# Where the rotation tables are loaded and worked out, and how the first weights come in, in a decoder block on one core

## The chip, the cores and the metric

The kernel runs on one core of a Trainium2 chip. A core has five engines with a queue of instructions each: TensorE (PE: matrix products and transposes), VectorE (DVE), ScalarE (ACT), GpSimd (POOL) and SyncE (SP, which here only issues DMAs). Engines run on their own and wait for each other by semaphores. The metric is the device time of one execution, in microseconds (us).

## The reference, cut to what matters

One block of a decoder for 1024 tokens of width 1024. Only the beginning of its first part, the two mixers, is touched:

```python
h = rms_norm(x, attn_norm_g)                 # x / sqrt(mean(x*x) + 1e-6) * g
proj = h @ w_in                              # 1024 x 3688, split by columns
dq, dk, dv, iq, ik, iw, cq, ckv, kpe, gd, gm = split(proj)
k_a = rope(rms_norm(dk, dsa_k_g), pos)       # 64 columns, first attention's key
k_i = rope(ik, pos)                          # 64 columns, indexer's key
kv_b = rms_norm(ckv, mla_ckv_g) @ mla_w_ukv  # 128 columns -> 8 heads x (64 + 64)
k_b = rms_norm(concat(k_nope, k_pe), mla_k_g)
def rope(x, pos):                            # rotation by pos * inv_freq
    cos, sin = cos(ang), sin(ang)
    return concat(x1 * cos - x2 * sin, x2 * cos + x1 * sin)
```

Behind it come attention over the 256 best keys, a second causal attention, gates, a cross attention to a memory and a mixture of 16 experts.

## The kernel before, in words

Every float32 product is made of three: each operand is split into a rounded high half (`hi`, ScalarE) and the rest (`lo`, VectorE or GpSimd), and TensorE multiplies hi by hi, hi by lo and lo by hi (`mm3`, L529 to L531).

The first stage is the loop at L809 in `prep`. It goes over eight tiles `i` of 128 tokens, skewed so that each pass works on several tiles at once. Each pass squares the next tile of x on ScalarE (`square_x`, L805), works out reciprocal square roots by three Newton steps in twelve short operations on VectorE (`newton`, L545 to L551), scales the tile (`xn`, L815), and transposes it in two halves on TensorE (L607), each split into `hT_hi` and `hT_lo` (L516, L517). One pass later `project` multiplies tile `i-1` by the 360 weight columns of the first chunk in 24 matmuls of 360 columns, and ScalarE copies the result out (`ev`, L766) and takes its squares (L831 to L834). Three passes behind, the columns of the keys are scaled and rotated with the tables of that tile (`tabs`, L771; `rope_on`, L723 to L726, on GpSimd), duplicated (`kd`, L852), transposed (L859, L861) and split (`cT`, `ks`, `ik`). Four passes behind, `cT` is multiplied by `mla_w_ukv` and copied to `kvb` (L876), and its squares are summed (L878, L879). Those sums, and the sums of the squares of `ev`, share the Newton chain of a later tile of x: `newton` of pass `i` takes eleven columns, of which the first belongs to x of tile `i`, two to `ev` of tile `i-3` and eight to `kvb` of tile `i-6`. So the scaling of tile 6 of x waits for the `kvb` of tile 0.

The 360 columns lie in three pieces of `w_in` (128, 72 and 160 columns). `chunk` loads them in 24 DMAs of 128 rows on SyncE's queue into four buffers `wr` in turn (L559), rounds on ScalarE (L520) and takes the rest on GpSimd (L521). The tables (`tables`, L661 to L719) are cosine and sine of position times frequency, with and without the gains `g_k`, `g_q`, `g_mk`, `g_mq`; they are written to memory as `d_tab` and read back tile by tile. Their small inputs are loaded on SyncE's queue in the middle of, and behind, the weight loads.

The code is written in the order of the loop. A scheduler then puts each engine's instructions into an order by estimated readiness; `issue_after(ins)` keeps instructions that are written inside it behind `ins`. Loads on SyncE's and ScalarE's queue take eight semaphores in turn: a load waits until the load that used its semaphore before has landed.

Of the kernel before, what the change touches and what calls it, by code (L numbers as in the profile page):

```python
# [9 lines left out]
F32 = mybir.dt.float32  # L10
F32R = mybir.dt.float32r
BF16 = mybir.dt.bfloat16
I32 = mybir.dt.int32
AF = mybir.ActivationFunctionType
OP = mybir.AluOpType
# [4 lines left out]
S, D, T, KD = 1024, 1024, 8, 8  # L20
# [478 lines left out]
class Hybrid:  # L499
# [9 lines left out]
    def row(self, name, off, n, tname, pool=None):  # L509
        t = (pool or self.cst).tile([128, n], F32, name=tname)  # L510
        src = self.I[name]
        self.nc.sync.dma_start(t, bass.AP(tensor=src.tensor, offset=src.offset + off, ap=[[0, 128], [1, n]]))
        return t

    def split(self, hi, lo, src):
        self.nc.scalar.activation(hi, src, AF.Copy)  # L516
        self.nc.vector.tensor_sub(lo, src, hi.bitcast(F32))  # L517

# [83 lines left out]
    def transpose_rows(self, xn, hi, lo):  # L602
        for h in range(2):
            p = self.tp().rearrange("p (a b) -> p a b", a=4)
            for i in range(4):
                k = 4 * h + i
                self.nc.tensor.transpose(p[:, i, :], xn[:, k * 128:(k + 1) * 128], self.ident)  # L607
            self.split(hi[:, 4 * h:4 * h + 4], lo[:, 4 * h:4 * h + 4], p)
# [52 lines left out]
    def tables(self, pool):  # L661
        nc, I = self.nc, self.I
        G = nc.gpsimd
        pi = pool.tile([128, T], I32, name="pos_i")
        p = I['positions']
        nc.sync.dma_start(pi, bass.AP(tensor=p.tensor, offset=p.offset, ap=[[1, 128], [128, T]]))
        inv = self.row('inv_freq', 0, 32, "inv", pool)
        gq = self.row('dsa_q_norm_g', 0, 64, "g_q", pool)
        nc.vector.tensor_scalar_mul(gq, gq, -0.125)
        gk = self.row('dsa_k_norm_g', 0, 64, "g_k", pool)  # L670
        mq = self.row('mla_q_norm_g', 64, 32, "g_mq", pool)
        mk = self.row('mla_k_norm_g', 64, 32, "g_mk", pool)
# [3 lines left out]
        ang, k = ak[:, 0], ak[:, 1]  # L676
# [51 lines left out]
    def prep(self):  # L728
# [8 lines left out]
        ikst = (hp.tile([128, S], F32R, name="ik_hi"), hp.tile([128, S], F32R, name="ik_lo"))  # L737
# [5 lines left out]
        W = I['w_in'][0]  # L743
# [47 lines left out]
        def load_x(t):  # L791
            xt[t] = xp.tile([128, D], F32, name="xt", bufs=3)
            (nc.sync if t < 3 else nc.gpsimd).dma_start(xt[t], I['x'][0, tk(t), :])

        load_x(0)
        grow = self.row('attn_norm_g', 0, D, "grow", xp)
        load_x(1)
# [6 lines left out]
        def square_x(t):  # L804
            A.activation(xj, xt[t], AF.Square, scale=1.0 / 32, accum_out=ms(t)[:, 0:1])  # L805

        A.activation(xj[:, 0:128], self.ident, AF.Square)
        square_x(0)
        for i in range(T + 7):  # L809
            if i + 1 < T:  # L810
                square_x(i + 1)
            y = self.newton(ms(i)[:, 0:11], (128, 11))
            if i < T:
                xn = xp.tile([128, D], F32, name="xn", bufs=2)
                V.scalar_tensor_tensor(xn, xt[i], y[:, 0:1], grow, op0=OP.mult, op1=OP.mult)  # L815
                self.transpose_rows(xn, hT[0][:, :, tk(i)], hT[1][:, :, tk(i)])
                if i + 2 < T:
                    load_x(i + 2)
            if i == 0:
                ws, n = chunk([(512, 640), (1152, 1224), (1480, 1640)])  # L820
                c3 = ExitStack()
                tp_ = c3.enter_context(tc.tile_pool(name="tb", bufs=1, side="right"))
                self.tables(tp_)
                c3.close()
                ukv = [self.wpiece([(I['mla_w_ukv'][0, :, j * 512:(j + 1) * 512], 0)], 512) for j in range(2)]
# [1148 lines left out]
```

## Time and profile before

| | |
|---|---|
| median of 3 runs | 1403.38 us (1400.67 to 1403.90) |
| profiled execution | 1405.94 us, span 1404.2 us |
| mean clock granted to TensorE | 0.953 of full |
| TensorE busy | 1239.8 us (88%) |
| VectorE busy | 949.2 us (68%) |
| ScalarE busy | 807.1 us (57%) |
| GpSimd busy | 436.0 us (31%) |

The span is the time between the first and the last record of the profile; the execution's own time is 1.74 us longer. In the timeline a row is one operation or several of one kind in a row (x2, x3): the start, the time of all of them, the engine, the line, and what they write and read. What stands in square brackets is how long the engine was idle before and what ended that. A `q` behind an engine's name is its queue of DMA issues; such a row is the time of the issue, not that of the transfer.

### The profile page before, as it was taken

The page shows a single profiled execution, that of the slowest core. Times are in us where ns is not written, and L with a number is a line of the kernel's source. Part 1 is how long each engine was busy: PE and PEld are TensorE (multiplying, and loading weights), DVE is VectorE, ACT ScalarE, POOL GpSimd, SP SyncE. Part 2 cuts the span into 40 slices and gives each one's busy share as a digit, 9 for nine tenths or more (in the row PEclk, how much of TensorE's full clock was granted, in tenths as well). Part 3 has the DMA queues.
Part 4 walks back from the last instruction along what each step waited for, and adds up shares of the span by engine and source line. Part 5 has one row for each costly group of instructions (what it writes and reads, how often), then busy time and mean ns, then how long its engine had stood idle before and what let it go on. Part 6 is the DMA issues. An engine that isn't in the chain of part 4 may idle for free.

```text
span 1404.2 us, 20787 instructions
## 1 busy us (share of the span) xinstructions
PE 1239.8 (88%) x6884; PEld 1038.2 (74%) x6885; DVE 949.2 (68%) x1963; ACT 807.1 (57%) x1667; POOL 436.0 (31%) x541
## 2 busy tenths in 40 slices
PE   5789899988899999999998999999999378999893
PEld 4678778777787778888776787787878257788772
DVE  7786865889999578778888465232367735677650
ACT  5453654887672388888998422033455334667652
POOL 4555200528884121221343221221223431111111
PEclk9899999999999999999999999999999689999987
DMA  6564102534334454436221234531021857899972
GB/s 201 144 190 137 42 20 82 156 113 155 125 117 150 153 173 151 142 134 208 69 78 61 75 110 138 199 85 38 31 91 60 293 220 232 278 314 304 277 215 36
DMA packets 145749, 203.54 MB, mean 145 GB/s; under 512 B 69824, under 2 KB 91072, under 8 KB 145632
## 3 DMA queue, kind: packets, MB, share of 16 engines
q1 hardware_dynamic: 137040, 173.22, 38.4%
q0 software_dynamic: 7440, 24.71, 6.5%
q10 hardware_dynamic: 1152, 4.19, 0.7%
q8 instruction: 56, 0.92, 0.3%
q14 instruction: 61, 0.50, 0.1%
HBM read 134.61 MB, written 69.70 MB: 146 GB/s over the span
## 4 chain that ended last, share of the span: by engine, by line
PE 36%; DVE 19%; ACT 12%; DMA 11%; issue 9%; POOL 3%; SPq 0%; DVEq 0%; ACTq 0%; POOLq 0%
PE acc L529 4%; PE acc L530 3%; PE acc L531 3%; PE s L529 3%; PE s L530 3%; PE s L531 3%; DMA dn_raw<-in_moe_w_down_dram 2%; ACT tk_junka L1200 2%; DVE ik_hi L1190 2%; DVE ik_lo L1190 2%; DMA gu_raw<-in_moe_w_up_dram 2%; PE tp L1356 2%; PE s L933 1%; DMA gu_raw<-in_moe_w_gate_dram 1%; PE acc L1370 1%
## 5 line engine op out<-in xcount | busy, mean ns | idle before, releaser
L521 POOL TENSOR_TENSOR wl<-wr,wh 128x512 fp32r<-128x512 f32 (+2 forms) x86 | 109.8, 1294 | 175.0 <-ACT wh L520 125.3
L517 DVE TENSOR_TENSOR PT_lo<-tp,PT_hi 128x512 fp32r<-128x512 f32 x152 | 101.6, 685 | 27.4 <-ACT PT_hi L516 26.2
L529 PE MATMUL s<-hT_hi,wh 128*128 128x512 f32 x256 | 102.9, 402 | 3.7 <-ACT s L1061 3.7
L1743 POOL DMA_INDIRECT out_dram<-ey,etok x24 | 39.5, 1644 | 210.4 <-ACT ey L1758 60.0
L531 PE MATMUL s<-hT_hi,wl 128*128 128x512 f32 x256 | 102.0, 401 | 1.7 <-POOL wl L521 1.7
L1726 DVE TENSOR_TENSOR gu_lo<-gu_raw,gu_hi 128x1024 fp32r<-128x1024 f32 x60 | 71.7, 1220 | 44.7 <-ACT gu_hi L1725 42.5
L530 PE MATMUL s<-hT_lo,wh 128*128 128x512 f32 x256 | 101.9, 401 | 0.0
L516 ACT ACTIVATE PT_hi<-tp 128x512 fp32r<-128x512 f32 x152 | 86.7, 594 | 20.3 <-PE tp L1356 8.5
L1200 ACT ACTIVATE tk_junka<-sc,tk_b 128x512 bf16<-128x512 f32 (+2 forms) x96 | 79.4, 827 | 30.5 <-DVE tk_b L1197 29.6
L520 ACT ACTIVATE wh<-wr 128x512 fp32r<-128x512 f32 (+2 forms) x86 | 50.8, 608 | 77.6 <-PE acc L531 27.7
L529 PE MATMUL acc<-wh,hT_hi 128*128 128x512 f32 (+2 forms) x240 | 86.0, 361 | 10.2 <-ACT ev L766 5.4
L1725 ACT ACTIVATE gu_hi<-gu_raw 128x1024 fp32r<-128x1024 f32 x60 | 62.2, 1056 | 50.6 <-DMA gu_raw<-in_moe_w_gate_dram 19.9
L531 PE MATMUL acc<-wh,hT_lo 128*128 128x512 f32 (+2 forms) x240 | 86.6, 361 | 1.9 <-DVE hT_lo L517 1.9
L530 PE MATMUL acc<-wl,hT_hi 128*128 128x512 f32 (+2 forms) x240 | 85.7, 358 | 0.5 <-POOL wl L521 0.5
L1338 DVE TENSOR_REDUCE low<-s 128x1 f32<-128x256 f32 (+3 forms) x64 | 49.1, 769 | 33.0 <-PE s L1337 32.8
L529 PEld LDWEIGHTS acc<-wh,hT_hi 128*128 128x128 f32 x240 | 47.6, 198 | 17.0 <-ACT hT_hi L516 6.0
L529 PEld LDWEIGHTS s<-hT_hi,wh 128*128 128x128 f32 x256 | 49.5, 193 | 14.2 <-ACT s L1061 4.4
L529 PE MATMUL s<-eT1h,gu_hi 128*128 128x224 f32 (+2 forms) x192 | 54.2, 282 | 5.4 <-DVE ewt L1689 3.4
L531 PEld LDWEIGHTS s<-hT_hi,wl 128*128 128x128 f32 x256 | 49.4, 193 | 12.0 <-POOL wl L521 2.1
L942 DVE SCALAR_TENSOR_TENSOR sc<-rel,iw,sc 128x384 f32<-128x384 f32 (+5 forms) x42 | 43.2, 1030 | 21.2 <-ACT rel L936 18.0
L530 PEld LDWEIGHTS s<-hT_lo,wh 128*128 128x128 f32 x256 | 49.6, 194 | 10.1
L530 PE MATMUL s<-eT1l,gu_hi 128*128 128x224 f32 (+2 forms) x192 | 54.6, 284 | 0.0
(543 smaller groups left out, 4126.2 us busy)
## 6 DMA issues: line engine op xcount, KB each, us to landing
d_xs<-zero SPq DMA_DIRECT2D x32, 516.0 KB
dn_raw<-in_moe_w_down_dram SPq DMA_DIRECT2D x32, 512.0 KB
gu_raw<-in_moe_w_gate_dram SPq DMA_DIRECT2D x30, 512.0 KB
gu_raw<-in_moe_w_up_dram SPq DMA_DIRECT2D x30, 512.0 KB
wr<-in_w_in_dram SPq DMA_DIRECT2D x48, 256.0 KB
d_g<-s SPq DMA_DIRECT2D x32, 256.0 KB
gt<-d_g SPq DMA_DIRECT2D x16, 512.0 KB
xg<-d_xs SPq DMA_DIRECT2D x13, 512.0 KB
```

The costliest lines, as they stand in the source:

```text
L516: self.nc.scalar.activation(hi, src, AF.Copy)
L517: self.nc.vector.tensor_sub(lo, src, hi.bitcast(F32))
L520: self.nc.scalar.activation(hi, src, AF.Copy)
L521: self.nc.gpsimd.tensor_sub(lo, src, hi.bitcast(F32))
L529: mm(out, a[0], b[0], start=start, stop=False)
L530: mm(out, a[0], b[1], start=False, stop=False)
L531: mm(out, a[1], b[0], start=False, stop=stop)
L1190: V.tensor_scalar(junks[0][:, :(t + 1) * 128], blk(t), b[:, i:i + 1].bitcast(F32), None, op0=op, op1=OP.add, accum_out=cnt[:, i:i + 1])
L1200: A.activation(junka[:, :(t + 1) * 128], blk(t), AF.Sign, bias=b[:, i:i + 1].bitcast(F32), accum_out=cnt[:, i:i + 1])
L1338: nc.vector.tensor_reduce(low[:, b:b + 1], sp[:, 0:nch, 0:w], AX.XY, OP.min)
L1725: A.activation(hi[:, z], raw_z, AF.Copy)
L1726: E.tensor_sub(lo[:, z], raw_z, hi[:, z].bitcast(F32))
```

## The change

- The seven inputs of the tables and of the normalisation (`pos_i`, `inv`, `grow` and four gains) are loaded by ScalarE's DMA queue, first of all on it, instead of SyncE's.
- The weights of the first chunk come in four pieces of 256 rows with three loads each, 12 instead of 24. They land in buffers that are not yet in use for their own purpose (two of `kvb`, and `ik_hi` and `ik_lo`), so none waits for a buffer to come free. The loads of tiles 1 and 2 of x stand between the pieces.
- The lower halves of these weights are taken alternately on GpSimd and VectorE; their rounding stands behind the first square of x.
- The tables are worked out behind the first normalised tile, the Newton steps of tile 1 too; the pieces of `mla_w_ukv` behind the last split of tile 0.

```diff
--- before.py
+++ after.py
@@ -506,15 +506,16 @@
         if self.dbg is not None and name in self.dbg:
             self.nc.sync.dma_start(self.dbg[name], ap)
 
-    def row(self, name, off, n, tname, pool=None):
+    def row(self, name, off, n, tname, pool=None, q=None):
         t = (pool or self.cst).tile([128, n], F32, name=tname)
         src = self.I[name]
-        self.nc.sync.dma_start(t, bass.AP(tensor=src.tensor, offset=src.offset + off, ap=[[0, 128], [1, n]]))
+        (q or self.nc.sync).dma_start(t, bass.AP(tensor=src.tensor, offset=src.offset + off, ap=[[0, 128], [1, n]]))
         return t
 
     def split(self, hi, lo, src):
-        self.nc.scalar.activation(hi, src, AF.Copy)
+        q = self.nc.scalar.activation(hi, src, AF.Copy)
         self.nc.vector.tensor_sub(lo, src, hi.bitcast(F32))
+        return q
 
     def split_pool(self, hi, lo, src):
         self.nc.scalar.activation(hi, src, AF.Copy)
@@ -605,7 +606,8 @@
             for i in range(4):
                 k = 4 * h + i
                 self.nc.tensor.transpose(p[:, i, :], xn[:, k * 128:(k + 1) * 128], self.ident)
-            self.split(hi[:, 4 * h:4 * h + 4], lo[:, 4 * h:4 * h + 4], p)
+            last = self.split(hi[:, 4 * h:4 * h + 4], lo[:, 4 * h:4 * h + 4], p)
+        return last
 
 
     def build(self):
@@ -658,18 +660,20 @@
         nc.vector.tensor_scalar(self.tri3[:, 128:256], jp, 0.0, -NEG, op0=OP.is_gt, op1=OP.mult)
         nc.vector.memset(self.tri3[:, 256:384], -NEG)
 
-    def tables(self, pool):
+    def table_inputs(self, pool, xp):
+        nc, I = self.nc, self.I
+        pi = pool.tile([128, T], I32, name="pos_i")
+        p = I['positions']
+        nc.scalar.dma_start(pi, bass.AP(tensor=p.tensor, offset=p.offset, ap=[[1, 128], [128, T]]))
+        inv = self.row('inv_freq', 0, 32, "inv", pool, nc.scalar)
+        grow = self.row('attn_norm_g', 0, D, "grow", xp, nc.scalar)
+        return grow, [pi, inv] + [self.row(*a, pool, nc.scalar) for a in (('dsa_k_norm_g', 0, 64, "g_k"), ('mla_k_norm_g', 64, 32, "g_mk"), ('dsa_q_norm_g', 0, 64, "g_q"), ('mla_q_norm_g', 64, 32, "g_mq"))]
+
+    def tables(self, pool, inputs):
         nc, I = self.nc, self.I
         G = nc.gpsimd
-        pi = pool.tile([128, T], I32, name="pos_i")
-        p = I['positions']
-        nc.sync.dma_start(pi, bass.AP(tensor=p.tensor, offset=p.offset, ap=[[1, 128], [128, T]]))
-        inv = self.row('inv_freq', 0, 32, "inv", pool)
-        gq = self.row('dsa_q_norm_g', 0, 64, "g_q", pool)
+        pi, inv, gk, mk, gq, mq = inputs
         nc.vector.tensor_scalar_mul(gq, gq, -0.125)
-        gk = self.row('dsa_k_norm_g', 0, 64, "g_k", pool)
-        mq = self.row('mla_q_norm_g', 64, 32, "g_mq", pool)
-        mk = self.row('mla_k_norm_g', 64, 32, "g_mk", pool)
         pf = pool.tile([128, T], F32, name="pos_f")
         nc.vector.tensor_copy(pf, pi)
         ak = pool.tile([128, T * 64], F32, name="ang").rearrange("p (a t f) -> p a t f", a=2, t=T)
@@ -734,7 +738,6 @@
         self.wp = c.enter_context(tc.tile_pool(name="wp", bufs=10))
         hp = c.enter_context(tc.tile_pool(name="hp", bufs=1))
         hT = self.hT = (hp.tile([128, KD, S], F32R, name="hT_hi"), hp.tile([128, KD, S], F32R, name="hT_lo"))
-        ikst = (hp.tile([128, S], F32R, name="ik_hi"), hp.tile([128, S], F32R, name="ik_lo"))
         iw = hp.tile([128, T, 8], F32, name="iw")
         wk = c.enter_context(tc.tile_pool(name="wk", bufs=2))
         cwe = ExitStack()
@@ -792,9 +795,20 @@
             xt[t] = xp.tile([128, D], F32, name="xt", bufs=3)
             (nc.sync if t < 3 else nc.gpsimd).dma_start(xt[t], I['x'][0, tk(t), :])
 
+        c3 = ExitStack()
         load_x(0)
-        grow = self.row('attn_norm_g', 0, D, "grow", xp)
-        load_x(1)
+
+        kcols, kraw = ((512, 640), (1152, 1224), (1480, 1640)), []
+        for h, (pool, nm) in enumerate(((kp, "kvb"), (hp, "ik_hi"), (kp, "kvb"), (hp, "ik_lo"))):
+            raw, o = pool.tile([128, S], F32, name=nm)[:, 0:720].rearrange("p (k n) -> p k n", k=2), 0
+            for a, b in kcols:
+                nc.sync.dma_start(raw[:, :, o:o + b - a], W[h * 256:h * 256 + 256, a:b].rearrange("(k p) n -> p k n", p=128))
+                o += b - a
+            kraw.append(raw)
+            if h % 2:
+                load_x(1 + h // 2)
+        tp_ = c3.enter_context(tc.tile_pool(name="tb", bufs=1, side="right"))
+        grow, tin = self.table_inputs(tp_, xp)
         ckv_row = self.row('mla_ckv_norm_g', 0, 128, "ckv_row", hp)
         cq_row = self.row('mla_cq_norm_g', 0, 256, "cq_row", hp)
         ms = Stats()
@@ -802,27 +816,35 @@
         xj = xp.tile([128, D], BF16, name="xj", bufs=1)
 
         def square_x(t):
-            A.activation(xj, xt[t], AF.Square, scale=1.0 / 32, accum_out=ms(t)[:, 0:1])
+            return A.activation(xj, xt[t], AF.Square, scale=1.0 / 32, accum_out=ms(t)[:, 0:1])
 
         A.activation(xj[:, 0:128], self.ident, AF.Square)
-        square_x(0)
+        first = square_x(0)
         for i in range(T + 7):
             if i + 1 < T:
                 square_x(i + 1)
-            y = self.newton(ms(i)[:, 0:11], (128, 11))
+            with tc.issue_after(last_xn.ins) if i == 1 else nullcontext():
+                y = self.newton(ms(i)[:, 0:11], (128, 11))
             if i < T:
                 xn = xp.tile([128, D], F32, name="xn", bufs=2)
-                V.scalar_tensor_tensor(xn, xt[i], y[:, 0:1], grow, op0=OP.mult, op1=OP.mult)
-                self.transpose_rows(xn, hT[0][:, :, tk(i)], hT[1][:, :, tk(i)])
-                if i + 2 < T:
+                last_xn = V.scalar_tensor_tensor(xn, xt[i], y[:, 0:1], grow, op0=OP.mult, op1=OP.mult)
+                rows_T = self.transpose_rows(xn, hT[0][:, :, tk(i)], hT[1][:, :, tk(i)])
+                if 2 < i + 2 < T:
                     load_x(i + 2)
             if i == 0:
-                ws, n = chunk([(512, 640), (1152, 1224), (1480, 1640)])
-                c3 = ExitStack()
-                tp_ = c3.enter_context(tc.tile_pool(name="tb", bufs=1, side="right"))
-                self.tables(tp_)
+                ws, n = [], 360
+                for k in range(KD):
+                    hi, lo = (self.wp.tile([128, 512], F32R, name=nm)[:, 0:n] for nm in ("wh", "wl"))
+                    with tc.issue_after(first.ins):
+                        A.activation(hi, kraw[k // 2][:, k % 2], AF.Copy)
+                    (V if k % 2 else G).tensor_sub(lo, kraw[k // 2][:, k % 2], hi.bitcast(F32))
+                    ws.append((hi, lo))
+                ikst = tuple(hp.tile([128, S], F32R, name=nm) for nm in ("ik_hi", "ik_lo"))
+                with tc.issue_after(first.ins), tc.issue_after(last_xn.ins):
+                    self.tables(tp_, tin)
                 c3.close()
-                ukv = [self.wpiece([(I['mla_w_ukv'][0, :, j * 512:(j + 1) * 512], 0)], 512) for j in range(2)]
+                with tc.issue_after(rows_T.ins):
+                    ukv = [self.wpiece([(I['mla_w_ukv'][0, :, j * 512:(j + 1) * 512], 0)], 512) for j in range(2)]
             t = i - 1
             if 0 <= t < T:
                 e = ev[t] = project(ws, n, t)
```

How the order of instructions changes shows at three places. In what follows `DMAHW0` to `DMAHW7` are the eight semaphores of the loads, and a name in square brackets is what the instruction waits for.

ScalarE at the program's start, before: the table load of its functions, a short square, the squares of x (`xj<-xt`) and the first roundings (`wh<-wr`).

```order
L807 ACT_TABLE_LOAD
L807 ACTIVATE xj<-ident 128x128 [waits DVE_49]
L805 ACTIVATE xj,ms<-xt 128x1024 [waits DMAHW0_49,Activation_49,Pool_49]
L805 ACTIVATE xj,ms<-xt 128x1024 [waits DMAHW2_49,Activation_49,Pool_49]
L805 ACTIVATE xj,ms<-xt 128x1024 [waits DMAHW5_49,Activation_49,Pool_49]
L520 ACTIVATE wh<-wr 128x360 [waits DMAHW7_49,DMAHW6_49,DMAHW0_49]
L520 ACTIVATE wh<-wr 128x360 [waits DMAHW3_49,DMAHW2_49,DMAHW1_49]
```

ScalarE at the same place, now:

```order
L667 DMA pos_i<-in_positions_dram 128x8x1
L512 DMA inv<-in_inv_freq_dram 128x32
L512 DMA grow<-in_attn_norm_g_dram 128x1024
L512 DMA g_k<-in_dsa_k_norm_g_dram 128x64
L512 DMA g_mk<-in_mla_k_norm_g_dram 128x32 [waits DMAHW1_49]
L512 DMA g_q<-in_dsa_q_norm_g_dram 128x64 [waits DMAHW3_49]
L512 DMA g_mq<-in_mla_q_norm_g_dram 128x32 [waits DMAHW5_49]
L821 ACT_TABLE_LOAD
L821 ACTIVATE xj<-ident 128x128 [waits DVE_49]
L819 ACTIVATE xj,ms<-xt 128x1024 [waits Activation_49,Pool_49]
L839 ACTIVATE wh<-kvb 128x360 [waits DMAHW6_49,DMAHW4_49,DMAHW2_49]
```

Seven loads stand in front of the table load; three of them wait for an earlier load: the fifth for that of the first tile of x on SyncE's queue, the sixth for `inv`, the seventh for `grow`.

VectorE at the end of the first Newton chain, up to the first normalised tile (`xn`), before:

```order
L551 SCALAR_TENSOR_TENSOR rq_y<-rq_t,rq_y 128x11 [waits DVE_49]
L549 TENSOR_TENSOR rq_t<-rq_y 128x11 [waits DVE_49]
L550 SCALAR_TENSOR_TENSOR rq_t<-rq_t,ms 128x11 [waits DVE_49]
L551 SCALAR_TENSOR_TENSOR rq_y<-rq_t,rq_y 128x11 [waits DVE_49]
L815 SCALAR_TENSOR_TENSOR xn<-xt,rq_y,grow 128x1024 [waits DMAHW1_49,DMAHW0_49,DVE_49]
```

VectorE there, now, from the fifth operation of the chain on (`wl` is the lower half of a weight piece):

```order
L840 TENSOR_TENSOR wl<-kvb,wh 128x360 [waits DMAHW4_49,DMAHW6_49,DMAHW2_49,Activation_49]
L551 SCALAR_TENSOR_TENSOR rq_t<-rq_t,ms 128x11 [waits DVE_49]
L552 SCALAR_TENSOR_TENSOR rq_y<-rq_t,rq_y 128x11 [waits DVE_49]
L840 TENSOR_TENSOR wl<-ik_hi,wh 128x360 [waits DMAHW2_49,DMAHW4_49,DMAHW0_49,Activation_49]
L550 TENSOR_TENSOR rq_t<-rq_y 128x11 [waits DVE_49]
L551 SCALAR_TENSOR_TENSOR rq_t<-rq_t,ms 128x11 [waits DVE_49]
L552 SCALAR_TENSOR_TENSOR rq_y<-rq_t,rq_y 128x11 [waits DVE_49]
L550 TENSOR_TENSOR rq_t<-rq_y 128x11 [waits DVE_49]
L551 SCALAR_TENSOR_TENSOR rq_t<-rq_t,ms 128x11 [waits DVE_49]
L552 SCALAR_TENSOR_TENSOR rq_y<-rq_t,rq_y 128x11 [waits DVE_49]
L840 TENSOR_TENSOR wl<-kvb,wh 128x360 [waits DMAHW1_49,DMAHW7_49,DMAHW0_49,Activation_49]
L830 SCALAR_TENSOR_TENSOR xn<-xt,rq_y,grow 128x1024 [waits DMAHW5_49,DVE_49]
```

Three weight splits are set among the short operations in front of the first normalised tile.

ScalarE around the first copy of the rotated key (`kd`) and the first `kvb`, before; the first row is the square of the last tile of x:

```order
L805 ACTIVATE xj,ms<-xt 128x1024 [waits DMASW4_49,Pool_49]
L516 ACTIVATE hT_hi<-tp 128x4x128 [waits PE_49]
L852 ACTIVATE kd<-kd 128x2x64 [waits Pool_49] x2
L516 ACTIVATE cT_hi<-tp 128x128 [waits PE_49] x2
L516 ACTIVATE ks<-tp 128x128 [waits DVE_49] x2
L516 ACTIVATE ik_hi<-tp 128x128 [waits DVE_49] x2
L766 ACTIVATE ev<-acc 128x360 [waits DMAHW1_49,PE_49]
L852 ACTIVATE kd<-kd 128x2x64 [waits Pool_49]
L876 ACTIVATE kvb<-s 128x1024 [waits PE_49]
```

ScalarE there, now:

```order
L516 ACTIVATE cT_hi<-tp 128x128 [waits PE_49]
L769 ACTIVATE ev<-acc 128x360 [waits PE_49]
L516 ACTIVATE ks<-tp 128x128 [waits DVE_49]
L516 ACTIVATE hT_hi<-tp 128x4x128 [waits PE_49]
L853 ACTIVATE s_605,ms<-ev 128x64 [waits Activation_49]
L854 ACTIVATE s_605,ms<-ev 128x128
L856 ACTIVATE s_605,sskpe<-ev 128x32
L516 ACTIVATE ik_hi<-tp 128x128 [waits DVE_49]
L874 ACTIVATE kd<-kd 128x2x64 [waits Pool_49]
L898 ACTIVATE kvb<-s 128x1024 [waits PE_49]
L819 ACTIVATE xj,ms<-xt 128x1024 [waits DMASW4_49]
L516 ACTIVATE hT_hi<-tp 128x4x128 [waits PE_49]
```

The square of the last tile of x (`xj,ms<-xt`) now stands behind the first `kvb`, and the copy of tile 0's key stands some rows ahead of what is shown here, ahead of the square of the seventh tile.

## Rows read from the trace of the kernel before

**Rows 1.** Page, part 1: busy time, share of the span and count.
```profile
PE 1239.8 (88%) x6884; PEld 1038.2 (74%) x6885; DVE 949.2 (68%) x1963; ACT 807.1 (57%) x1667; POOL 436.0 (31%) x541
```

**Rows 2.** Windows of 10 us: length, PE, PEld, DVE, ACT, POOL busy, clock, DMA, GB/s.
```profile
0.00:10.00 10.00, 0.19 (x1) 0.20 (x3) 4.46 (x22) 3.95 (x8) 0.82 (x13) 1.00 0.71 257
...
50.00:60.00 10.00, 9.12 (x40) 8.70 (x41) 3.25 (x11) 4.46 (x14) 5.75 (x24) 0.67 0.36 106
...
80.00:90.00 10.00, 10.00 (x61) 9.39 (x60) 7.12 (x18) 7.40 (x21) 4.98 (x15) 0.98 0.50 120
```

**Rows 3.** Timeline of ScalarE: start, length, line, operation, out<-in, [idle before <-releaser].
```profile
0.76 1.28 ACT L807 ACT_TABLE_LOAD   x1 [0.63 <-PEq L1961]
2.06 0.31 ACT L807 ACTIVATE xj<-ident 128x128 bf16<-128x128 f32 x1
4.83 1.06 ACT L805 ACTIVATE xj<-xt 128x1024 bf16<-128x1024 f32 x1 [2.47 <-DMA xt<-in_x_dram]
...
26.47 0.49 ACT L520 ACTIVATE wh<-wr 128x360 fp32r<-128x360 f32 x1
...
51.79 1.06 ACT L805 ACTIVATE xj<-xt 128x1024 bf16<-128x1024 f32 x1 [4.13 <-DMA xt<-in_x_dram]
...
53.33 0.50 ACT L852 ACTIVATE kd<-kd 128x128 f32<-128x128 f32 x2
...
59.72 1.03 ACT L876 ACTIVATE kvb<-s 128x1024 f32<-128x1024 f32 x1 [0.73 <-PE s L531]
```

**Rows 4.** Timeline of VectorE.
```profile
8.27 0.17 DVE L551 SCALAR_TENSOR_TENSOR rq_y<-rq_t,rq_y 128x11 f32<-128x11 f32 x1
8.47 1.28 DVE L815 SCALAR_TENSOR_TENSOR xn<-xt,rq_y,grow 128x1024 f32<-128x1024 f32 x1
...
11.64 1.00 DVE L549 TENSOR_TENSOR rq_t<-rq_y 128x11 f32<-128x11 f32 x2
...
14.52 0.68 DVE L517 TENSOR_TENSOR hT_lo<-tp,hT_hi 128x512 fp32r<-128x512 f32 x1
...
22.49 0.41 DVE L686 SCALAR_TENSOR_TENSOR ang<-ang 128x256 f32<-128x256 f32 x1
...
61.44 0.69 DVE L879 TENSOR_REDUCE ms<-s 128x8 f32<-128x512 f32 x1 [2.44 <-ACT s L878]
...
67.14 2.02 DVE L815 SCALAR_TENSOR_TENSOR xn<-xt,rq_y,grow 128x1024 f32<-128x1024 f32 x1
...
72.09 1.28 DVE L815 SCALAR_TENSOR_TENSOR xn<-xt,rq_y,grow 128x1024 f32<-128x1024 f32 x1
```

**Rows 5.** Timeline of TensorE.
```profile
28.78 0.33 PE L531 MATMUL acc<-wh,hT_lo 128*128 128x360 f32 x1
...
75.60 0.48 PE L859 MATMUL tp<-ident,cn 128*128 128x128 f32 x1 [3.47 <-DVE hT_lo L517]
...
88.19 0.33 PE L531 MATMUL acc<-wh,hT_lo 128*128 128x360 f32 x1
...
135.60 0.39 PE L529 MATMUL acc<-wh,hT_hi 128*128 128x256 f32 x1 [2.14 <-ACT ev L766]
```

**Rows 6.** Timeline of SyncE's DMA queue.
```profile
3.69 8.41 SPq L559 DMA_DIRECT2D wr<-in_w_in_dram  x12
...
19.70 0.43 SPq L512 DMA_DIRECT2D g_k<-in_dsa_k_norm_g_dram  x1
...
42.05 1.00 SPq L771 DMA_DIRECT2D tabs<-d_tab  x2
```

**Rows 7.** Timeline of GpSimd.
```profile
11.59 2.78 POOL L521 TENSOR_TENSOR wl<-wr,wh 128x360 fp32r<-128x360 f32 x3 [0.76 <-ACT wh L520]
...
46.45 0.48 POOL L723 TENSOR_TENSOR kt<-x,tabs 128x128 f32<-128x128 f32 x1
```

**Rows 8.** Waits of SyncE's queue, 0 to 22 us: total, times, longest.
```profile
SPq L559 <- DMA grow<-in_attn_norm_g_dram: 1.2, 1, 1.2
```

**Rows 9.** Timeline of SyncE's queue from 5.8 us.
```profile
6.52 2.63 SPq L559 DMA_DIRECT2D wr<-in_w_in_dram  x4
```

## The prediction

> **What bounds the kernel now.** I read the page first: TensorE is busy 1239.8 of the span's 1404.2 us [rows 1]. So a change in one stage pays only where TensorE stands still or runs below full clock. The change touches only the first stage, so next come the windows of 10 us over its 135 us [rows 2]: in the first ten TensorE does 0.19 us of work, between 50 and 60 it is busy at a granted clock of 0.67, from 80 on it is full. The chip has two levels, 1.2 and 2.4 GHz; 0.67 is a stretch that is mostly at the lower one.
>
> Then the timelines, engine by engine, to see what arrives last. Head: the first square of x starts at 4.83, when tile 0 of x has landed [rows 3]; VectorE's short operations follow and the first normalised tile starts at 8.47 [rows 4]. TensorE's matmuls of tile 0 then wait for weights: the last weight piece is rounded by ScalarE only at 26.47 [rows 3], and tiles 0 and 1 end together at 28.78 [rows 5]. Middle: the rotation tables. Their gain rows are issued by SyncE at 19.70, behind 24 weight loads that take it from 3.69, and the finished tables come back at 42.05 [rows 6]. GpSimd begins to rotate the first key at 46.45 [rows 7], ScalarE copies the rotated key at 53.33, the evicted product kvb of tile 0 starts at 59.72 [rows 3], VectorE sums its squares at 61.44, and only behind that sum, in the same chain of short operations, do the normalised tiles 6 (67.14) and 7 (72.09) come [rows 4]. TensorE waits 3.47 us at 75.60 for the split of tile 7, ends tile 7's product at 88.19, and reaches the point where the two programs' orders meet again, the eight-step product of 256 columns, at 135.60 [rows 5]. What ends last in this stage is therefore that chain of tables, kvb and the tiles 6 and 7, more than the weights.
>
> **The change, part by part.**
>
> *Seven loads on ScalarE's queue.* ScalarE issues positions, inv_freq, grow and four gain rows before its table load. No row shows an issue on ScalarE; on SyncE one took 0.43 (g_k) to 0.50 (two of tabs in 1.00) [rows 6], and I take 0.43. Even at twice that the first four would be out by 4.2, and nobody waits for them, since the fifth waits until x0 has landed (4.8, when the first square began), the sixth for inv_freq, the seventh for grow. The order shows these as waits for the landing of the load issued eight before; that SyncE stood in the same way before shows in its wait for grow. This is the added wait. Behind it on ScalarE stand the table load (1.28), a short square of 0.31 [rows 3], the first square of x and every rounding of the weights, and behind those VectorE and TensorE. SyncE stood 1.2 us for grow [rows 8] and went on at 6.52 [rows 9]; grow now goes out some 0.8 later, in the same traffic, so I let the last issue end at 7.1 (6.5 to 8.0), and the first square starts at 7.1 + 1.28 + 0.31 = 8.7, 3.9 later than 4.83.
>
> *Weight loads.* 24 issues become 12, of 256 rows each. SyncE spent 8.41 on the first twelve [rows 6], so some 10 us of its queue goes. The first ten microseconds already carry 257 GB/s at 71% of the DMA engines [rows 2], so what is won is the queue and not the transfer: I cost it at nothing for the head, and take what comes from the last weight piece (26.47) no longer bounding tile 0. The Trainium skill, page "DMA: Bandwidth & Descriptors", section "Issuing engines are not separate DMA queues", says that loads started by different engines run on the same 16 DMA engines and interleave, so a second issuing engine saves only the issue. By that rule too the seven loads on ScalarE would slow x0 and the weights by their bytes and bring nothing but the earlier issue; the trace's 257 GB/s out of one queue agrees.
>
> *Half the weight splits on VectorE.* Of eight lower halves GpSimd keeps four (0.93 each: 2.78 for three [rows 7]); VectorE gets four of 128x360, three of them among the twelve short operations that give the first normalised tile. No row shows one: the nearest are 0.41 (128x256) below and 0.68 (128x512) above [rows 4]; I take 0.50, so 1.5 us in front of that tile. The upper bound is that each also waits for a GpSimd split: the short operations in [rows 4] took 1.00 for two while GpSimd split weights, against 0.17 for one alone, so up to 0.93 each, 3.8 in all. ScalarE has to round six pieces (0.49 each [rows 3]) and square x1 (1.06) before the third of them. Earliest start of the tile: 8.7 + 1.06 + 6 x 0.49 + 1.06 + 0.5 = 14.3; with all of the lock 14.3 + 3.8 = 18.1. I take 15.5, nearer to the lower end because ScalarE's roundings space the splits out; that is 7.0 later than 8.47.
>
> *Tile 0's products.* Transposes and splits took 6.0 from the tile's start at 8.47 to the split at 14.52 [rows 4]; with 15.5 the split is ready near 20, and 24 matmuls (the weights are there by now) end at 26 to 27, some 2 earlier than 28.78. Tile 1 loses: VectorE works out the angles and the interleaved chains of tiles 1 and 2 first, so that its product ends at 39 instead of 28.78 (an estimate from walking the order of the changed kernel with these durations, as are the next). By tile 4 both kernels are level: TensorE's idle time between 30 and 60 takes the delay up.
>
> *Tables and kvb.* With the inputs in hand the sine work follows the first normalised tile, and the tables are written and read back before tile 0's key is scaled. So the rotation no longer waits for tables but for VectorE's chain of tile 3, which gives tile 0's factors, near 42. Between the rotation's start at 46.45 and the copy at 53.33 lay the rotations of two tiles, 3.4 for each at most; I take 3.0, so the copy comes at 45. From the copy to kvb was 59.72 - 53.33 = 6.4 [rows 3], so kvb starts at 51.4, 8.3 earlier. ScalarE's order helps: the copy stands ahead of the square of tile 6 instead of behind that of tile 7, which waited for x until 51.79 [rows 3]. The sum is then at 53.1 and tile 6 at 53.1 + 5.7 = 58.8, 8.3 earlier. Tile 7 waits in addition for the buffers and splits of tile 6: 66.5 against 72.09, 5.6 earlier. Before, 3.47 of waiting [rows 5] and a low clock followed it; with the product of kvb of tile 0 already done ahead of tile 4 there is work for TensorE there, and I take 4.1 of it back. Tile 7's product ends at 78.5: 9.7 earlier.
>
> *What is given back.* Between 88.19 and 135.60 lie 47.4 us in which TensorE is nearly always busy; these stay. But a stretch like 50 to 60, ten microseconds at 0.67, costs 10 x 0.33 = 3.3 [rows 2], and the longer idle head and VectorE's crowded 15 to 35 make one more of them likely. I take 3.2 off.
>
> **Sum.** 1405.94 (the profiled execution, 1.74 outside its span) - 9.7 + 3.2 = 1399.4. That execution lies 2.56 above the median of 1403.38, so the median comes to 1396.9: **1397**, 6.5 faster. Bounds for this case: the clock takes 0 to 3.3 and the first tile starts between 14.3 and 17, which moves kvb by some of that: -10 to -4.2, so 1393 to 1399.
>
> **Rivals.**
>
> *All of it is kept.* No further cold stretch, and VectorE's splits fit between GpSimd's: 9.7 plus up to 2 from tile 0's earlier end. 1403.38 - 11.7 = 1391.7. For it: TensorE's 3.47 at 75.60 [rows 5] and the stretch at 0.67 [rows 2] are there to be taken. Against: the late head.
>
> *The lock takes it.* Each of VectorE's weight splits waits behind a GpSimd one, 3.8 more at the first tile, and the delay goes with VectorE's chain through to kvb (55.2) and tile 7. Left: 6.5 - 3.8 = 2.7, 1400.7: within what can be told from no change (0.3%, 4.2 us). The price is the row of 1.00 for two short operations. The Trainium skill, page "SBUF — State Buffer", section "Who interferes with whom", says that a VectorE operation with both inputs in SBUF contends with a GpSimd one that reads SBUF. A weight split is of that form; by the rule this rival's wait is certain and only its length is open.
>
> *The late head stays (slower).* One mechanism: ScalarE stands in its queue until grow has landed, every later square, rounding and eviction comes 4 to 7 us late, and the tables, worked out on the same VectorE behind the first tile, delay tile 1 and 2 so that the chain through kvb does not come earlier. It decides at kvb of tile 0: if that starts at 59.72 or later, tiles 6 and 7 are no earlier, and of the head's 7.0 some 4 to 5 stay, the rest hidden by the wait of 3.47: 1403.38 + 4.6 = 1408. For it: tile 1's product 10 later. Against: the keys stood still for the tables alone until 46.45.
>
> *A load that was hidden anyway.* Nothing in the stage waits for x7: it lands by 51.79 [rows 3], and tile 7 is normalised at 72.09. That the loads of x keep their times is no gain and no loss; it is in no sum.
>
> **How the numbers follow.** Forecast 0.40, all kept 0.15, lock 0.27, late head 0.18. Above 0.3% faster: 0.40 + 0.15 = 0.55; within 0.3%: 0.27; slower: 0.18. The range reaches from 1387 (all kept, with another 5 from a head without waits) to 1408, where the late head's price lies; the forecast's own range is 1393 to 1399.
>
> **What would show it.** ScalarE's first square of x at 8 to 9.5 with its loads standing before it; the first normalised tile at 14 to 17; VectorE's splits 0.5 long (lock: 1.0 and more); tile 0's product done before 28, tile 1's near 39; GpSimd's first rotation at 42 to 44; kvb of tile 0 at 50 to 53; tiles 6 and 7 at 59 and 66; the product of 256 columns at 129 instead of 135.60, and this difference kept to the end. I am wrong if kvb is not before 57, or if it is and the product of 256 columns is still reached after 133.

## The result, and the profile after

The changed kernel takes 1394.24 us in the median against 1403.64, ratio 0.9931 (95% interval 0.9911 to 0.9952): 9.4 us faster. Its profiled execution takes 1393.33 us, span 1391.6. One of its eight executions took 1440.89 us at a granted clock of 0.83 and is left out of the ratio.

First ScalarE's timeline of the changed kernel; columns as in [rows 3].

```profile
7.96 0.40 ACTq L512 DMA_DIRECT2D g_mq<-in_mla_q_norm_g_dram  x1
8.39 1.28 ACT L821 ACT_TABLE_LOAD   x1 [8.27 <-DMA g_q<-in_dsa_q_norm_g_dram]
...
10.09 1.06 ACT L819 ACTIVATE xj<-xt 128x1024 bf16<-128x1024 f32 x1
...
46.03 0.31 ACT L874 ACTIVATE kd<-kd 128x128 f32<-128x128 f32 x1 [1.96 <-POOL kd L730]
...
53.39 1.03 ACT L898 ACTIVATE kvb<-s 128x1024 f32<-128x1024 f32 x1
```

ScalarE's queue stands until `grow` has landed, and the last issue goes out at 7.96. The first square comes at 10.09 instead of 4.83, and still the copy of the first `kvb` starts 6.3 earlier than in [rows 3]. VectorE's timeline of the changed kernel:

```profile
11.90 0.80 DVE L550 TENSOR_TENSOR rq_t<-rq_y 128x11 f32<-128x11 f32 x1
12.62 0.52 DVE L840 TENSOR_TENSOR wl<-kvb,wh 128x360 fp32r<-128x360 f32 x1
...
16.95 1.97 DVE L830 SCALAR_TENSOR_TENSOR xn<-xt,rq_y,grow 128x1024 f32<-128x1024 f32 x1
...
56.58 0.68 DVE L901 TENSOR_REDUCE ms<-s 128x8 f32<-128x512 f32 x1
...
61.22 2.17 DVE L830 SCALAR_TENSOR_TENSOR xn<-xt,rq_y,grow 128x1024 f32<-128x1024 f32 x1
...
69.28 2.17 DVE L830 SCALAR_TENSOR_TENSOR xn<-xt,rq_y,grow 128x1024 f32<-128x1024 f32 x1
```

The first normalised tile is 8.5 later than in [rows 4], tile 6 is 5.9 and tile 7 is 2.8 earlier. TensorE's timeline of the kernel before, two lines that [rows 5] does not have:

```profile
105.12 0.33 PE L859 MATMUL tp<-ident,cn 128*128 128x128 f32 x1 [2.44 <-DVE cn L843]
...
143.26 1.09 PE L1150 MATMUL tp<-ident,dup 128*128 128x128 f32 x8 [1.70 <-ACT dup L919]
```

TensorE's timeline of the changed kernel:

```profile
81.35 0.33 PE L532 MATMUL acc<-wh,hT_lo 128*128 128x360 f32 x1
...
100.51 0.33 PE L881 MATMUL tp<-ident,cn 128*128 128x128 f32 x1 [0.30 <-DVE cn L865]
...
121.28 0.28 PE L530 MATMUL acc<-wh,hT_hi 128*128 128x256 f32 x1
...
124.16 0.36 PE L530 MATMUL acc<-wh,hT_hi 128*128 128x256 f32 x1
...
132.79 1.09 PE L1172 MATMUL tp<-ident,dup 128*128 128x128 f32 x8 [2.59 <-ACT dup L941]
```

Tile 7's product ends at 81.35 (88.19 in [rows 5]). Behind it the transposition of a late key (`cn`) waits 0.30 instead of 2.44. There are three products of 256 columns in a row. The first begins at 121.28 instead of 130.42, the second at 124.16 instead of 135.60 (the line in [rows 5] is that of the second, behind a wait of 2.14 that is gone now). The first transposition of the queries (`dup`), which I take as the stage's end from here on, comes at 132.79 instead of 143.26: 10.5 earlier. At 788 us of the span before, the distance is 9.8, at 1143 it is 8.3, at the end of the span 12.6: it is kept.

The windows show where TensorE gained; columns as in [rows 2]. Two of the kernel before that [rows 2] does not have:

```profile
30.00:40.00 10.00, 6.57 (x32) 6.31 (x32) 9.35 (x36) 5.93 (x28) 5.26 (x9) 0.83 0.65 177
...
70.00:80.00 10.00, 5.76 (x25) 5.14 (x24) 9.30 (x31) 3.78 (x9) 6.83 (x18) 0.68 0.54 157
```

The same of the changed kernel, with the one that answers to 50 to 60 in [rows 2]:

```profile
30.00:40.00 10.00, 7.38 (x32) 7.00 (x33) 8.37 (x26) 3.64 (x7) 4.26 (x6) 0.66 0.80 221
...
50.00:60.00 10.00, 8.74 (x46) 7.07 (x47) 9.02 (x34) 7.30 (x25) 4.50 (x14) 1.00 0.50 141
...
70.00:80.00 10.00, 8.64 (x51) 7.28 (x50) 9.58 (x27) 6.47 (x20) 7.15 (x18) 1.00 0.45 128
```

Before, three stretches of the stage lay well below full clock (0.83, 0.67, 0.68), and 70 to 80 held 5.76 of work; now one is left (0.66, 30 to 40), and 70 to 80 holds 8.64. Up to the stage's end TensorE was idle 35.9 before and 30.0 after, and busy 107.4 and 102.8 with as many matmuls. So of the 10.5 us some 5.9 are idle time, and 4.6 are less busy time for the same number of matmuls, as three stretches of low clock have become one. No run moves the clock alone.

### The profile page after: what moved, and what is told of

Its sections match the earlier page's. It is cut to its first block, busy times and chain, and to the rows that moved or that the text cites. A ratio compares the mean times of both kernels' runs of the same rounds, so it can differ in the third digit from the quotient of the medians.

```text
span 1391.6 us, 20751 instructions
## 1 busy us (share of the span) xinstructions
PE 1237.9 (89%) x6884; PEld 1036.9 (75%) x6885; DVE 949.3 (68%) x1967; ACT 806.8 (58%) x1667; POOL 440.1 (32%) x537
## 4 chain that ended last, share of the span: by engine, by line
PE 48%; DVE 19%; ACT 12%; DMA 11%; issue 6%; POOL 2%; SPq 1%; DVEq 0%; ACTq 0%; POOLq 0%
PE acc L530 5%; PE acc L531 5%; PE acc L532 5%; PE s L530 4%; PE s L531 4%; PE s L532 4%; DMA gu_raw<-in_moe_w_gate_dram 2%; ACT tk_junka L1222 2%; PE tp L1378 2%; PE s L955 2%; DVE ik_hi L1212 1%; PE tp L1475 1%; DVE ik_lo L1212 1%; PE acc L1392 1%; PE acc L1391 1%
## 5 line engine op out<-in xcount | busy, mean ns | idle before, releaser
L522 POOL TENSOR_TENSOR wl<-wr,wh 128x512 fp32r<-128x512 f32 (+1 forms) x78 | 102.2, 1328 | 164.1 <-ACT wh L521 120.4
L516 ACT ACTIVATE PT_hi<-tp 128x512 fp32r<-128x512 f32 x152 | 86.8, 594 | 21.5 <-PE tp L1475 9.6
L1222 ACT ACTIVATE tk_junka<-sc,tk_b 128x512 bf16<-128x512 f32 (+2 forms) x96 | 79.4, 827 | 28.0 <-DVE tk_b L1219 27.0
L521 ACT ACTIVATE wh<-wr 128x512 fp32r<-128x512 f32 (+1 forms) x78 | 47.0, 619 | 73.2 <-PE acc L532 27.8
L530 PE MATMUL acc<-wh,hT_hi 128*128 128x512 f32 (+2 forms) x240 | 85.2, 356 | 0.2 <-ACT hT_hi L516 0.2
L530 PE MATMUL acc<-wh,mg_hi 128*128 128x512 f32 x128 | 52.4, 415 | 3.1 <-issue 3.1
```

Of the source, the lines that this page charges most:

```text
L516: q = self.nc.scalar.activation(hi, src, AF.Copy)
L522: self.nc.gpsimd.tensor_sub(lo, src, hi.bitcast(F32))
L530: mm(out, a[0], b[0], start=start, stop=False)
L1222: A.activation(junka[:, :(t + 1) * 128], blk(t), AF.Sign, bias=b[:, i:i + 1].bitcast(F32), accum_out=cnt[:, i:i + 1])
```

## The experiments

| kernel | kvb of tile 0: rows of its halves on TensorE | starts at | tile 7 ends | stage ends | ratio to before (95%) |
|---|---|---|---|---|---|
| before | 130, 133 | 59.7 | 88.2 | 143.3 | 1 |
| changed | 107, 110 | 53.4 | 81.4 | 132.8 | 0.9931 (0.9911-0.9952) |
| e1_no_head_wait | 119, 122 | 59.7 | 85.2 | 143.1 | 0.9968 (0.9950-0.9985) |
| e2_old_weight_loads | 106, 120 | 62.4 | 88.7 | 139.0 | 1.0001 (0.9983-1.0019) |
| e3_weights_alone | 119, 122 | 51.5 | 77.1 | 136.5 | 0.9943 (0.9920-0.9965) |
| e4_splits_gpsimd | 106, 109 | 57.8 | 84.7 | 136.5 | 0.9934 (0.9920-0.9949) |
| e5_tables_later | 132, 134 | 60.9 | 88.2 | 139.8 | 0.9976 (0.9960-0.9993) |
| e6_24_loads | 108, 122 | 58.6 | 84.9 | 136.8 | 0.9911 (0.9886-0.9936) |
| e8_tables_alone | 107, 121 | 60.2 | 86.4 | 138.8 | 0.9945 (0.9921-0.9969) |
| e9_sine_first | 106, 109 | 54.3 | 81.1 | 132.8 | 0.9913 (0.9886-0.9939) |
| e10_weights_key_first | 106, 109 | 48.3 | 78.9 | 132.4 | 0.9943 (0.9921-0.9965) |
| e11_key_first | 106, 110 | 53.7 | 83.6 | 134.7 | 0.9934 (0.9919-0.9950) |
| e12_sine_key_first | 106, 109 | 51.2 | 79.4 | 131.1 | 0.9898 (0.9882-0.9914) |
| e13_kvb_after_tile4 | 135, 138 | 60.8 | 88.1 | 143.2 | 1.0009 (0.9992-1.0025) |

The times come from one profiled execution each, the ratios from 5 to 12 executions of a kernel. The second column gives the places of the first matmul of each half in TensorE's written order; several matmuls of one kind in a row are one place. The code cuts are abridged.

**Does the wait on ScalarE cost its 5 us?** Three loads move to SyncE:

```diff
-  return grow, [pi, inv] + [self.row(*a, pool, nc.scalar) for a in (g_k, g_mk, g_q, g_mq)]
+  return grow, [pi, inv, self.row(g_k, pool, nc.scalar)]   # g_mk, g_q, g_mq on SyncE behind cq_row
```

> The changed kernel, with the three gain rows whose issue waits on ScalarE's queue (g_mk, g_q, g_mq) put on SyncE's queue behind cq_row; ScalarE issues four loads that wait for nothing. First square of x at 4.8 to 5.5 (changed kernel 10.09), first normalised tile at 11 to 13 (16.95). Theory A (the end of the stage is set by the chain tables, key, kvb of tile 0, normalised tiles 6 and 7; the late head lies beside it): kvb of tile 0 moves by less than 3 us and the time stays within 2 us of the changed kernel's, ratio to the kernel before 0.992 to 0.995. Theory B (the late head is paid in full): 4 to 5 us more are won, ratio 0.989 to 0.990.

The first square comes at 4.58, and yet about half of the gain is lost: that is neither theory A (kvb of tile 0 moves by more than 6 us) nor theory B. The traces of this kernel say why the middle is late, GpSimd first, then ScalarE and VectorE:

```profile
15.12 0.79 POOL L796 DMA_DIRECT2D xt<-in_x_dram  x1 [1.61 <-DVE ms L546]
```

```profile
23.82 1.06 ACT L820 ACTIVATE xj<-xt 128x1024 bf16<-128x1024 f32 x1 [5.32 <-DMA xt<-in_x_dram]
...
25.51 1.28 ACT L696 ACT_TABLE_LOAD   x1
```

```profile
28.48 0.37 DVE L713 TENSOR_TENSOR ang<-tC,g_mk 128x128 f32<-128x128 f32 x1 [3.90 <-ACT tC L699]
```

ScalarE stands 5.32 for tile 3 of x with the sine work queued behind its square, and VectorE 3.90 for the table. So one run turns the two round:

```diff
+  with tc.issue_after(self.sine_done.ins) if i == 2 else nullcontext():
       square_x(i + 1)
```

> The kernel without the wait on ScalarE (e1_no_head_wait) with one thing moved: the square of tile 3 stands behind the sine work on ScalarE instead of ahead of it; in that run ScalarE stood 5.32 us for x of tile 3 with the sine work behind it, and VectorE 3.90 us for the table. Theory G (that queue order is why taking the head's wait away lost 4 us): the sine work starts at 21 to 22 instead of 25.5, kvb of tile 0 at 54 to 57 instead of 59.66, ratio 0.991 to 0.994. Rival (VectorE's order between the third normalised tile and the fourth, and GpSimd's query tables ahead of the first key, set it): kvb stays at 58 to 60, ratio 0.996 to 0.998.

The ratio is 0.9913, as theory G had it. The first square comes 5.3 us earlier than in the changed kernel and the first normalised tile 3.7 earlier (13.27), and still the stage ends at the same 132.8: in this kernel the late head is hidden, and without it nothing is won that is clear of noise. But TensorE's order changed with this edit too (119, 122 to 106, 109), so the order of ScalarE's queue is not shown to be all of it.

**Which part brings the gain?** The weight part undone (old `chunk`), then alone (`grow` and the table inputs on SyncE, nothing held), then the table part alone (four small loads on ScalarE, `grow` behind x0, old `chunk`):

> The changed kernel with the weight part undone: 24 loads of 128 rows into the four buffers in turn, all lower halves on GpSimd; the table inputs on ScalarE's queue and what is held behind the first tile stay. Theory A (tables and key chain): kvb of tile 0 stays at or before 55 (before 59.72, changed 53.39) and most of the gain stays, ratio 0.993 to 0.997. Theory C (the gain is the weights', through SyncE's queue and the four splits taken from GpSimd): no gain or a loss, since the late head stays without what pays for it, ratio 1.000 to 1.004.

> The weight part alone: 12 loads into the borrowed buffers and splits in turn on GpSimd and VectorE; grow on SyncE's queue behind x0, the table inputs on SyncE's queue behind the weights (issued near 14 to 18 us), nothing held behind the first tile. First square of x at 4.8. Theory A: it depends on when the tables are there; the inputs land near 18 and the sine work comes some microseconds later than in the changed kernel, kvb of tile 0 at 53 to 57, ratio 0.993 to 0.998. Theory C: the whole gain, 0.990 to 0.994, whether kvb comes early or not.

> The table part alone and without the wait on ScalarE: the weight loads, buffers and splits of the kernel before; grow on SyncE's queue behind x0; positions, inv_freq, g_k and g_mk on ScalarE's queue, g_q and g_mq on SyncE's ahead of the weights; what is held behind the first tile as in the changed kernel. First square at 4.8. Theory A (tables early are enough): kvb of tile 0 at 52 to 56, ratio 0.993 to 0.996. Theory D (SyncE's queue, by way of the weights): tile 0's product still ends near 28 to 31 with the weights, kvb gains 2 to 4 us at most, ratio 0.997 to 1.000.

Either part alone gives most of the gain, and the table part with the wait on ScalarE gives none. In e2 the first square comes at 12.27 and tile 0's product is copied at 39.7 (27.6 changed). That the late head meets late weights there is a reading; no run separates the two. In e8 the time is what theory A gave, but not by its way, since kvb is no earlier than in the kernel before:

```profile
60.19 1.03 ACT L885 ACTIVATE kvb<-s 128x1024 f32<-128x1024 f32 x1 [0.34 <-PE s L532]
```

Up to the end of tile 7's product e8 gains 1.8, and from there to the stage's end another 2.7. For e3, SyncE issues the last gain row at 13.47, six microseconds earlier than `g_k` in [rows 6], so that the tables come as early there without ScalarE's queue.

**Loads, splits, tables one by one.** e6 puts 24 loads of 128 rows into the same buffers; e4 takes GpSimd (`G`) for all lower halves; e5 calls `tables` behind the third normalised tile:

```diff
-  (V if k % 2 else G).tensor_sub(lo, ...)      # e4
+  G.tensor_sub(lo, ...)
-  with tc.issue_after(first.ins), tc.issue_after(last_xn.ins): self.tables(tp_, tin)   # e5
+  if i == 2:                                    # in the third pass
+      with tc.issue_after(last_xn.ins): self.tables(tp_, tin)
```

> The changed kernel with the number of loads undone alone: 24 loads of 128 rows each instead of 12 of 256, into the same borrowed buffers, everything else kept. Theory D (what is won is SyncE's queue: twelve issues of 0.43 us and the waits for a free buffer, which brought weights and table inputs late before): the last weight load goes out some 5 us later, tile 0's product ends at 29 to 31 instead of 27.6, and a third to a half of the gain goes: ratio 0.995 to 0.998. Theory F (the buffers and the split between GpSimd and VectorE matter, the number of loads doesn't, since the bytes are the same): as the changed kernel, 0.992 to 0.995.

> The changed kernel with all eight lower halves on GpSimd, as before the change; TensorE's order stays that of the changed kernel. Theory: the first normalised tile comes at 14.5 to 16 instead of 16.95 (no split of 0.52 among the short operations), GpSimd ends its splits 2 to 4 us later, tile 0's product at 28 to 30 instead of 27.6; since the late head is not paid, the time stays, ratio 0.991 to 0.995. Rival (the sharing is needed): tile 0's product 3 us or more later and with it kvb, ratio 0.996 to 0.999.

> The changed kernel with one thing moved: the tables are worked out behind the third normalised tile instead of the first; their inputs are loaded as early as in the changed kernel. Theory A: the tables come back some 8 to 12 us later, kvb of tile 0 near 60 again, and the gain goes with it: ratio 0.998 to 1.003. Theory C (weights) and a theory of the early loads alone: no change from the changed kernel, 0.992 to 0.995.

The number of loads is worth nothing (0.9911). Nor is the sharing of the splits (0.9934), though with all of them on GpSimd tile 0's product is copied at 33.3 instead of 27.6 and kvb starts 4.5 later: these came late as the rival had it, and the time stayed as the theory had it. Tables later lose two thirds: kvb goes behind tile 4 in TensorE's order and starts at 60.9.

**Is it TensorE's order?** One edit to the changed kernel holds the product of the first kvb behind tile 4's. For that the whole block of this kvb (its product, its copy, its sum) is written one pass later, together with that of tile 1; loads, tables and splits stay:

```diff
-  t = i - 4
-  if 0 <= t < T:
+  for t in {4: (), 5: (0, 1)}.get(i, (i - 4,)):     # tile 0 in the pass of tile 1
+      with tc.issue_after(proj_last.ins) if t == 0 else nullcontext():   # last matmul of tile 4's product
           for j in range(2): self.mm3(pu[:, j], cT, ukv[j], True, True)
```

> The changed kernel with TensorE's order alone put back at one place: the product of kvb of tile 0 is held behind the whole product of tile 4, as in the kernel before, where both first kvb products stood together; loads, tables, splits and everything up to there stay. Theory H (half of the gain comes from this order, which the scheduler chose because keys come early: kvb's products and the products of tiles in turn): kvb of tile 0 back to 57 to 60, tile 7's product at 85 to 88, ratio 0.996 to 0.999. Theory of the loads alone: as the changed kernel, 0.992 to 0.995.

All of the gain is gone, more than theory H had. Up to the place of the edit the traces of this kernel and of the changed one hold the same operations in the same order: the first 135 on TensorE, 74 on ScalarE, 131 on VectorE and 79 on GpSimd. Behind it the order of all four differs, so what the edit moved is not TensorE's order alone. Timelines of this kernel, ScalarE first, then VectorE and TensorE:

```profile
44.86 0.31 ACT L875 ACTIVATE kd<-kd 128x128 f32<-128x128 f32 x1 [1.09 <-POOL kd L730]
...
60.84 1.02 ACT L902 ACTIVATE kvb<-s 128x1024 f32<-128x1024 f32 x1
```

```profile
62.56 0.69 DVE L905 TENSOR_REDUCE ms<-s 128x8 f32<-128x512 f32 x1 [2.43 <-ACT s L904]
...
68.30 1.28 DVE L830 SCALAR_TENSOR_TENSOR xn<-xt,rq_y,grow 128x1024 f32<-128x1024 f32 x1
...
72.25 1.30 DVE L830 SCALAR_TENSOR_TENSOR xn<-xt,rq_y,grow 128x1024 f32<-128x1024 f32 x1
```

```profile
75.26 0.47 PE L882 MATMUL tp<-ident,cn 128*128 128x128 f32 x1 [2.58 <-DVE hT_lo L517]
...
88.11 0.33 PE L532 MATMUL acc<-wh,hT_lo 128*128 128x360 f32 x1
...
104.83 0.33 PE L882 MATMUL tp<-ident,cn 128*128 128x128 f32 x1 [2.41 <-DVE cn L866]
...
143.18 1.09 PE L1176 MATMUL tp<-ident,dup 128*128 128x128 f32 x8 [1.54 <-ACT dup L945]
```

The key is copied at 44.86, earlier than in the changed kernel, but kvb starts at 60.84, and from there every line answers to one of the kernel before within 1.2 us: tiles 6 and 7 at 68.30 and 72.25, waits of 2.58 and 2.41, the stage's end at 143.18. In the table the six kernels with both halves at 110 or before end the stage at 131.1 to 136.5, the other eight at 136.5 to 143.3.

So in the changed kernel the early kvb is a condition of the gain. Its place in TensorE's order does not carry the gain alone: e1 and e3 have the same places (119, 122) and ratios of 0.9968 and 0.9943; e2, e6 and e8 have nearly the same (106 to 108, 120 to 122) and 1.0001, 0.9911 and 0.9945. What makes the difference among these is not shown.

**Can more be had?** The query tables (four operations on GpSimd, four on VectorE) behind the first rotated key, on the changed kernel, on e3 and on e9:

```diff
+  if t == 0:
+      with tc.issue_after(roped.ins), tc.issue_after(scaled_k.ins): query_tables()
```

> The changed kernel with the query tables behind the first rotated key. Theory A: copy of the key at 42 to 44 instead of 46.03, kvb at 50 to 52 instead of 53.39, tile 7's product 1 to 2 us earlier, ratio 0.991 to 0.993. Rival: no change, 0.992 to 0.995.

> The kernel with the weight part alone (e3_weights_alone) with one thing moved: the query tables (GpSimd four operations, 3.8 us, VectorE four) are worked out behind the first rotated key and not ahead of it. Theory A in its last form (the key chain of tile 0 sets tile 7's product): the copy of the key at 40 to 41.5 instead of 43.97, kvb at 48 to 49 instead of 51.45, tile 7's product at 74 to 75 instead of 77.1, and the time falls by 2 to 3 us, ratio 0.991 to 0.993. Rival (behind tile 7 TensorE only waits longer for the key of tile 6, 4.69 us in e3_weights_alone): tile 7's product earlier, but the time as e3_weights_alone, ratio 0.993 to 0.996.

> The kernel of e9_sine_first (no wait on ScalarE, sine work ahead of the square of tile 3) with the query tables behind the first rotated key. Theory A with H: copy of the key at 42 to 43 instead of 45.57, kvb at 51 to 52, TensorE's order as in the changed kernel, stage end 1 to 3 us earlier than the 132.8 of e9_sine_first, ratio 0.989 to 0.992. Rival (by then TensorE is full from 60 on, and what is left is idle time ahead of 40): as e9_sine_first within 1 us.

On the first two the time stays. On e9 it gives the kernel with the lowest median, 1389.69 us, 0.9898 (0.9882 to 0.9914), 13.4 us faster than before; its stage ends at 131.1. The interval overlaps that of e9 (0.9886 to 0.9939), so the last edit's own worth is not shown.

Open: what is won by the stage's end and what is won in the median differ by 4 to 6 us in e1, e2 and e6 (e6 ends the stage 6.4 earlier and takes 12.5 less), and e10 ends the stage 4.1 earlier than e3 at the same ratio. A profiled execution can lie that far from its median (e1's took 1403.29 against 1399.75, e4's 1401.42 against 1395.24), and the order of some later neighbours differs too; no run separates the two.

## Why the prediction was right, and where not

- *What bounds the stage*: right for the changed kernel. The chain kvb, sum, tiles 6 and 7 sets it; e13 shows it by taking the early kvb alone back. It is not all that counts: e8 gains with kvb at 60.19.
- *Head*: the mechanism as told, mis-sized. `grow` landed 6.1 after its issue, the first square came at 10.09 (8.7 forecast), the first tile at 16.95 (15.5). It cost nothing at the end, as forecast, so far as e9 shows it.
- *Weight loads at nothing*: right in price, 24 loads cost no more than 12 (e6). By the Trainium skill's rule in "DMA: Bandwidth & Descriptors", "Issuing engines are not separate DMA queues", issuing is usually small beside the transfer; e6 agrees.
- *VectorE's splits at 0.50*: 0.52 and 0.53. The lock fell on the short operations (0.80 to 0.90 for one) and on GpSimd's own splits (1.14 and 1.23 for two of them, 0.95 alone); GpSimd's first two in the changed kernel:

```profile
11.72 0.95 POOL L840 TENSOR_TENSOR wl<-kvb,wh 128x360 fp32r<-128x360 f32 x1 [10.35 <-DMA ik_hi<-in_w_in_dram]
12.80 1.14 POOL L840 TENSOR_TENSOR wl<-ik_hi,wh 128x360 fp32r<-128x360 f32 x1
```

  The Trainium skill, "SBUF — State Buffer", "Who interferes with whom", has such pairs contend; by that rule the rival's wait was there, and the trace agrees. It came to about 2 in front of the first tile (three short operations, each some 0.7 longer than 0.17), and in e9 that tile comes 3.7 earlier while the stage ends no earlier. The rival's 3.8 was summed too high: three splits stand in front of the tile, and 0.93 for each is 2.8.
- *Tile 0's products*: 15.5 and 6.0 make 21.5 and not 20. The second split came at 22.15, and the product was copied at 27.60 (its end was forecast at 26 to 27).
- *Tables and kvb*: copy of the key 46.03 (45 forecast), kvb 53.39 (51.4), tile 6 61.22 (58.8), tile 7 69.28 (66.5), tile 7's end 81.35 (78.5). The gain at that point is 6.8, not 9.7.
- *What is given back*: this step failed, in both of its parts. I took the 47.4 us behind tile 7 as staying, and took 3.2 off for one more stretch at the lower clock. There are two fewer, and of the waits behind tile 7 (2.44, 2.14 and 1.70 up to the stage's end) 0.30 and 2.59 are left, so that 3.6 more are won by there. Forecast 6.5, measured 9.4: two errors of opposite sign, 2.9 and 6.8, of which the second is the larger. That the time still lies in the stated range, near its lower end, is in part luck. The two errors give 10.4 at the stage's end, as measured there (10.5); the median moved by 1 less.
- The reading of 135.60 as the beginning of the 256-column product was wrong: that line is the second of the three such products.
- What the prediction did not see: that the gain of the changed kernel hangs on the scheduler's setting kvb of tile 0 ahead of tile 4. It named the place ("with the product of kvb of tile 0 already done ahead of tile 4") as a help and not as the condition that e13 shows it to be.

## What to carry to other kernels

Where a scheduler writes the order, read the place of the critical chain's link in the order of the engine it runs on, before pricing loads and waits: with the same early inputs the changed kernel won 9 us with that link ahead of the next tile and nothing with it held behind (e13). The place is a condition and not a price: with nearly the same place three kernels here lie between 1.0001 and 0.9911. An edit's own saving (12 loads, a wait of 5 us) may be worth nothing that is clear of noise. Test such a place by holding one product, and look in the trace for what else has moved.

## What was not expected of the hardware

- Tile 3 of x, issued on GpSimd's queue at 15.12 (e1), was there for ScalarE at 23.82; issued at 19.24 (changed kernel) at 23.66. Four microseconds earlier brought nothing. Weight loads were issued at the same time in both (from 14.2 us on in the changed kernel, from 14.5 in e1); whether they are the cause is not shown.
- An issue on ScalarE's queue took 0.33 to 0.60.
- With all lower halves on GpSimd (e4), one short operation of VectorE took 3.98 instead of 0.17; GpSimd was at its splits and an issue from 19.47 to 24.56. Why it lasted so long is not shown.

```profile
20.62 3.98 DVE L547 TENSOR_SCALAR rq_s<-ms 128x11 int32<-128x11 int32 x1
```
